# A decoder step on one core: in the recurrence's side work, the chunk products move ahead of the transpose of the decoded columns, and three pauses get longer

## The chip, the core and the metric

One core of a Trainium2 chip runs the whole program. The metric is the device time of one execution in microseconds (us); lower is better.

## The reference, cut to what is computed

One layer of a hybrid decoder, float32, for one prompt of 256 tokens and 8 decode rows (264 columns in all): a SwiGLU, a mixer, an attention over 256 memory tokens and a second SwiGLU, each with a layer norm behind it. The mixer is what matters here:

```python
proj = h @ p['w_in']                       # 2048 -> 3*1024 + 64 + 64 + 160 + 2*1024
r, k, v, wd, ad, gd = split(token_shift(proj[..., :SHIFT_COLS]))
# per head (16 heads of 64), per token t:
sa = einsum('bhvk,bhk->bhv', S, -kk_t)
S  = S * w_t[:, :, None, :] + sa[..., None] * (kk_t * a_t)[:, :, None, :] + v_t[..., None] * k_t[:, :, None, :]
y_t = einsum('bhvk,bhk->bhv', S, r_t)
o_a = ((group_norm(y) + bonus) * g)
u = glu(proj[..., SHIFT_COLS:])            # conv module: 31 taps along the tokens
o_b = silu(layer_norm(conv(u)))
merged = concatenate([o_a * beta_rwkv, o_b * beta_conv], -1) @ p['w_out']
```

## The kernel before, in words

Every weight matrix is read once, in chunks of 128x1024. ACT rounds a chunk to `whi` (L188) and DVE forms the rest `wlo` (L189); four such pairs are in store, three raw chunks ahead of them. Each product of activations and weights is three TensorE matmuls, `xh*whi`, `xl*whi` and `xh*wlo` (L303, L304, L305), 128x128 weights against 264 columns. I call these the large products and number them by their place on PE. A chunk is used by 24 of them.

The mixer first does the products with `w_in`, up to number 8784. As they go, 16 heads in four groups of four (g = 0 to 3) run the recurrence in chunked form as side work: small matmuls into one of four PSUM buffers (`mis`), with ACT and DVE work between them. For one group `rw_state` makes gates and scaled copies (`sig`, `a`, `E1`, `bk`, `ar`), the chunk products `G` (`gram`, L886, sixteen 128x128 matmuls, then four masked copies L890 on DVE), the transposed copies `bkT` (L825) and the solve of a triangular system, four rounds of L843 and L850 of 64 tiny matmuls each. `decode_rows` transposes the columns of the 8 decode rows (L1010) so that they can go through a DMA to `rw_decodes`. Then come the chain over the four chunks (`rw_chain`), the read (`rw_read`) and the group norm (`rw_out`, L1087 to L1106). The conv module's taps are DVE work (L1176), and its layer norm and Silu (`conv_apply`: L372 and L376 to L409, then L1200 and L1201) make the inputs k = 8 to 15 of the product with `w_out`.

That product, from number 8784, goes over four groups of 512 outputs. Within one it takes the inputs k = 0 to 5 (from groups 0 to 2), then 8 to 15 (conv). The inputs 6 and 7 come from group 3 and are taken last, from number 9288, so that group 3 can end in the meantime. Behind the product stand the residual (L1237, L1240, L1243) and the attention, whose memory rows come back by DMA (L1327) and are split again (L1328, L1329).

The order on each engine is set by the program. The main work yields a cost, which advances a clock `t`; each side has a time `next` at which it may issue its next piece, and a piece yields the pause until the following one:

```python
def step(self, now):
    self.next = now + self.pace * next(self.gen)
def pump(self):
    for s in self.sides:
        while not s.done and s.next <= self.t: s.step(self.t)
```

So a longer `yield` puts more large products ahead of what follows it. Before the product with `w_out` starts, groups 0 to 2 and the group norm of group 2 are issued to their ends (`self.finish(...)` in `mixer_out`); the sides of group 3 go on within it.

Of the kernel before, what the change touches and what calls it, by code (L numbers as in the profile page):

```python
# [12 lines left out]
ALU = mybir.AluOpType  # L13
# [14 lines left out]
C = 64  # L28
NC = TP // C
NP = 2 * NC  # L30
# [23 lines left out]
class Builder:  # L54
# [663 lines left out]
    def rw_state(self, g, S):  # L718

        nc = self.nc  # L720
        V, A = nc.vector, nc.scalar
# [15 lines left out]
        c8 = lambda t: t[:, :, :TP].rearrange("p i (c t) -> p i c t", t=C)  # L737
        e8 = lambda t, lo: t.rearrange("p (i c) t -> p i c t", i=2)[:, :, :, lo : lo + C]
# [38 lines left out]
        E1, E2 = L, Lc  # L777
# [11 lines left out]
        ar = S["ar"] = self.mt("ar", (128, NP, 2, C))  # L789
        bk = self.mt("bk", (128, 2, NC, 2, C))  # L790
        v8 = lambda t: t.rearrange("p (i c) t -> p i c t", i=2)
# [18 lines left out]
        r = S["r"]  # L810
        V.tensor_tensor(q[:, 1], q[:, 2], r[:, :, dec], ALU.mult)
        V.tensor_tensor(q[:, 5], a[:, :, dec], r[:, :, dec], ALU.mult)
        V.tensor_tensor(q[:, 6], k[:, :, dec], r[:, :, dec], ALU.mult)
        self.decode_rows(g, S)
        S["y"] = self.mt("y", (128, 2, T), bufs=2)
        self.decs.append(self.start(self.chain_after(self.decs[-1], self.rw_decodes(g, S)), DEC_PACE))
        V.tensor_tensor(v8(ar[:, :, 1]), c8(r), e8(E1, 1), ALU.mult)
        G = S["G"] = self.mt("G", (128, 2, NP, 2, C))
        self.gram(S)
        yield 1.0  # L820
        bkT = S["bkT"] = self.mt("bkT", (128, 2, NC, 128))
        for i in range(2):
            p = self.misc()
# [8 lines left out]
        mask = lambda l, o=slice(0, 128): self.lm[o, l, None].to_broadcast([o.stop - o.start, NP, B]).bitcast(I32)  # L832
        N = lambda n, c: G[QS[n], n // 2, c, 0, B * (n % 2) : B * (n % 2) + B]
        for n, o in enumerate(QS):
            V.copy_predicated(Q[o, :, 1], mask(0, o), N(n, slice(None)))
        V.transpose(Q[:, :, 0], Q[:, :, 1])
        yield 1.0
        b8 = lambda p: p[:, : B * NP].rearrange("p (c t) -> p c t", t=B)
        for l in range(1, 5):
            pp = b8(self.misc())  # L840
# [16 lines left out]
        for c in range(NP):  # L857
            for i in range(2):
                mm(pp[QS[2 * i + 1], c], G[QS[2 * i], i, c, 0, B:], Q[QS[2 * i], c, 0], start=True, stop=True)
        Pm = self.mt("P", (128, NP, B))  # L860
# [16 lines left out]
    def gram(self, S):  # L877
# [3 lines left out]
        for i in range(2):  # L881
# [7 lines left out]
            for h, p in enumerate(ps):  # L889
                nc.vector.tensor_tensor(  # L890
                    S["G"][:, i, NC * h : NC * h + NC],
                    p.rearrange("p c (a t) -> p c a t", t=C),
# [4 lines left out]
    def rw_chain(self, g, S):  # L897
# [17 lines left out]
        Z = S["Z"] = self.mt("Z", (128, NC + 1, 2, C))  # L915
        G, ar, bkT, QT = S["G"], S["ar"], S["bkT"], S["QT"]
        W2 = 2 * C
        h2 = lambda p: p[:, :W2].rearrange("p (h t) -> p h t", h=2)
        p = self.misc()
        for n in range(NP):  # L920
            for i in range(2):
                mm(p[HS[i], C * n : C * n + C], G[HS[1 - i], i, n, 0], UV[HS[1 - i], i, n], start=True, stop=True)
        W0 = self.mt("W0", (128, 2, NC, C))
# [41 lines left out]
    def rw_read(self, g, S):  # L965
# [14 lines left out]
        y = S["y"]  # L980
        G, ar, UV, Z = S["G"], S["ar"], S["UV"], S["Z"]
        p = self.misc()
# [891 lines left out]
```

## Time and profile before

| what | value |
|---|---|
| median of three runs | 2525.59 us (2519.16, 2527.02, 2525.59) |
| the profiled execution, its own time | 2526.33 us |
| span of its trace, first to last instruction | 2524.6 us |
| mean granted TensorE clock | 0.993 of full speed |
| PE busy | 2470.9 us, 98% |
| DVE, ACT, POOL busy | 1582.8, 1195.0, 261.7 us |
| products with `w_in` and the recurrence | about 840 to 1199 us of the span |
| product with `w_out` | about 1199 to 1340 us |

PE is busy nearly all the time, so the place to look is the stretches in which it is not, what released it there, and the granted clock. Matmuls are pipelined, so a row's duration is longer than its share of PE's time; large products follow each other every 0.12 us.

### The profile page before, as it was taken

The page shows a single profiled execution, that of the slowest core. Times are in us where ns is not written, and L with a number is a line of the kernel's source. Part 1 is how long each engine was busy: PE and PEld are TensorE (multiplying, and loading weights), DVE is VectorE, ACT ScalarE, POOL GpSimd, SP SyncE. Part 2 cuts the span into 40 slices and gives each one's busy share as a digit, 9 for nine tenths or more (in the row PEclk, how much of TensorE's full clock was granted, in tenths as well). Part 3 has the DMA queues.
Part 4 walks back from the last instruction along what each step waited for, and adds up shares of the span by engine and source line. Part 5 has one row for each costly group of instructions (what it writes and reads, how often), then busy time and mean ns, then how long its engine had stood idle before and what let it go on. Part 6 is the DMA issues. An engine that isn't in the chain of part 4 may idle for free. (4 is left out here: it accounts for less than half of the span.)

```text
span 2524.6 us, 53420 instructions
## 1 busy us (share of the span) xinstructions
PE 2470.9 (98%) x22328; PEld 2417.2 (96%) x22328; DVE 1582.8 (63%) x2545; ACT 1195.0 (47%) x1802; POOL 261.7 (10%) x422
## 2 busy tenths in 40 slices
PE   9999999999999999999989999999999999999998
PEld 9999999999999988988889888989999999999998
DVE  5545444444557599799777566789655545554465
ACT  5444433444446555455646354657444434444443
POOL 1300000000000001000110222220132500000000
PEclk9999999999999999999999999999999999999999
DMA  7656655555557754544476799976677755655554
GB/s 228 188 183 220 203 183 182 183 183 178 179 181 212 221 151 132 149 131 139 128 251 224 262 293 305 322 226 191 195 215 217 237 182 184 183 178 183 176 180 131
DMA packets 452211, 497.89 MB, mean 197 GB/s; under 512 B 22096, under 2 KB 418640, under 8 KB 451968
## 3 DMA queue, kind: packets, MB, share of 16 engines
q1 hardware_dynamic: 417840, 417.09, 54.0%
q0 software_dynamic: 20992, 67.22, 8.4%
q10 hardware_dynamic: 13136, 10.15, 1.2%
q8 instruction: 175, 2.87, 0.5%
q14 instruction: 68, 0.56, 0.1%
HBM read 477.76 MB, written 16.63 MB: 196 GB/s over the span
## 5 line engine op out<-in xcount | busy, mean ns | idle before, releaser
L189 DVE TENSOR_TENSOR wlo<-raw,whi 128x1024 fp32r<-128x1024 f32 (+1 forms) x791 | 961.4, 1216 | 850.6 <-ACT whi L188 847.3
L188 ACT ACTIVATE whi<-raw 128x1024 fp32r<-128x1024 f32 (+1 forms) x791 | 823.0, 1041 | 1035.6 <-PE acc L304 856.6
L303 PE MATMUL acc<-xh,whi 128*128 128x264 f32 x2864 | 828.7, 290 | 15.3 <-DVE y L1243 7.3
L304 PE MATMUL acc<-xl,whi 128*128 128x264 f32 x2864 | 820.2, 287 | 0.6 <-DVE xl L189 0.6
L305 PE MATMUL acc<-xh,wlo 128*128 128x264 f32 x2864 | 816.7, 286 | 0.5 <-DVE wlo L189 0.5
L303 PEld LDWEIGHTS acc<-xh,whi 128*128 128x128 f32 x2864 | 540.3, 189 | 23.8 <-ACT rh L1328 7.5
L304 PEld LDWEIGHTS acc<-xl,whi 128*128 128x128 f32 x2864 | 542.0, 189 | 3.7 <-DVE xl L189 0.8
L305 PEld LDWEIGHTS acc<-xh,wlo 128*128 128x128 f32 x2864 | 541.0, 189 | 2.3 <-DVE wlo L189 1.1
L303 PE MATMUL acc<-rh,whi 128*128 128x264 f32 (+2 forms) x1600 | 456.8, 285 | 0.2 <-ACT lnx L397 0.2
L305 PE MATMUL acc<-rh,wlo 128*128 128x264 f32 (+2 forms) x1600 | 454.5, 284 | 0.0
L304 PE MATMUL acc<-rl,whi 128*128 128x264 f32 (+2 forms) x1600 | 453.4, 283 | 0.0
L304 PE MATMUL acc<-gl,whi 128*128 128x264 f32 x1408 | 400.2, 284 | 0.0
L305 PE MATMUL acc<-gh,wlo 128*128 128x264 f32 x1408 | 400.1, 284 | 0.0
L303 PE MATMUL acc<-gh,whi 128*128 128x264 f32 x1408 | 399.5, 284 | 0.0
L303 PEld LDWEIGHTS acc<-rh,whi 128*128 128x128 f32 x1600 | 300.8, 188 | 2.2 <-ACT lnx L397 0.4
L304 PEld LDWEIGHTS acc<-rl,whi 128*128 128x128 f32 x1600 | 301.7, 189 | 1.2
L305 PEld LDWEIGHTS acc<-rh,wlo 128*128 128x128 f32 x1600 | 300.7, 188 | 0.2
L305 PEld LDWEIGHTS acc<-gh,wlo 128*128 128x128 f32 x1408 | 264.5, 188 | 0.1
L304 PEld LDWEIGHTS acc<-gl,whi 128*128 128x128 f32 x1408 | 264.5, 188 | 0.0
L303 PEld LDWEIGHTS acc<-gh,whi 128*128 128x128 f32 x1408 | 264.3, 188 | 0.1
L1176 DVE SCALAR_TENSOR_TENSOR y<-u,cw,y 128x256 f32<-128x256 f32 x240 | 111.1, 476 | 0.6
L397 ACT ACTIVATE lnx<-acc 128x264 f32<-128x264 f32 x84 | 32.4, 386 | 64.8 <-PE acc L305 64.8
(350 smaller groups left out, 2089.9 us busy)
## 6 DMA issues: line engine op xcount, KB each, us to landing
raw<-in_ffn_w SPq DMA_DIRECT2D x509, 512.0 KB, 3.6
raw<-in_w_in SPq DMA_DIRECT2D x86, 512.0 KB, 3.8
raw<-in_w_mk SPq DMA_DIRECT2D x32, 512.0 KB, 3.4
raw<-in_w_mv SPq DMA_DIRECT2D x32, 512.0 KB, 5.4
raw<-in_w_out SPq DMA_DIRECT2D x32, 512.0 KB, 5.1
kv<-in_cache_mem_k POOLq DMA_DIRECT2D x32, 512.0 KB, 6.2
raw<-in_w_mq SPq DMA_DIRECT2D x32, 512.0 KB, 5.2
kv<-in_cache_mem_v POOLq DMA_DIRECT2D x32, 512.0 KB, 6.1
```

Of the source, the lines that this page charges most:

```text
L188: a = self.nc.scalar.activation(hi, src, AF.Copy)
L189: return a, self.nc.vector.tensor_tensor(lo, src, hi.bitcast(F32), ALU.subtract)
L303: nc.tensor.matmul(out, wh, xh, start=start, stop=False)
L304: nc.tensor.matmul(out, wh, xl, start=False, stop=False)
L305: self.mark = nc.tensor.matmul(out, wl, xh, start=False, stop=stop)
L397: self.lastfn = self.nc.scalar.activation(*args, **kw)
L1176: V.scalar_tensor_tensor(c[:, :TP], u[:, i : i + TP], w(i), c[:, :TP], ALU.mult, ALU.add)
```

## The change

In `rw_state`, the product `ar[:, :, 1]` = r\*E1 (L817) and `gram` now come before `decode_rows`, with a pause of 2.2 between; the pause ahead of the `bkT` transposes is 2.4 instead of 1.0, and the one ahead of the solve 2.6 instead of 1.0. The chunk products used to follow the decoded columns with no pause.

```diff
@@ -811,13 +811,15 @@
         V.tensor_tensor(q[:, 6], k[:, :, dec], r[:, :, dec], ALU.mult)
+        V.tensor_tensor(v8(ar[:, :, 1]), c8(r), e8(E1, 1), ALU.mult)
+        yield 2.2
+        G = S["G"] = self.mt("G", (128, 2, NP, 2, C))
+        self.gram(S)
+
         self.decode_rows(g, S)
         S["y"] = self.mt("y", (128, 2, T), bufs=2)
         self.decs.append(self.start(self.chain_after(self.decs[-1], self.rw_decodes(g, S)), DEC_PACE))
-        V.tensor_tensor(v8(ar[:, :, 1]), c8(r), e8(E1, 1), ALU.mult)
-        G = S["G"] = self.mt("G", (128, 2, NP, 2, C))
-        self.gram(S)
-        yield 1.0
+        yield 2.4
         bkT = S["bkT"] = self.mt("bkT", (128, 2, NC, 128))
@@ -834,7 +836,7 @@
         V.transpose(Q[:, :, 0], Q[:, :, 1])
-        yield 1.0
+        yield 2.6
         b8 = lambda p: p[:, : B * NP].rearrange("p (c t) -> p c t", t=B)
```

Lines behind the change have numbers higher by two in the changed kernel (L886 becomes L888, L1010 becomes L1012); the text keeps the numbers of before. PE, DVE, POOL and SP issue the same instructions as before, in another order, and ACT two more table loads (L403). The table gives the number of large products ahead of each piece on PE, before and after:

| piece | group 0 | group 1 | group 2 | group 3 |
|---|---|---|---|---|
| L886, chunk products | 7317 -> 7318 | 7784 -> 7830 | 8282 -> 8337 | 8744 -> 8856 |
| L1010, decoded columns | 7312 -> 7318 | 7779 -> 7830 | 8277 -> 8342 | 8738 -> 8892 |
| L825, bkT | 7317 -> 7320 | 7784 -> 7836 | 8282 -> 8358 | 8744 -> 8916 |
| L843, first of the solve | 7339 -> 7358 | 7807 -> 7896 | 8304 -> 8394 | 8766 -> 8940 |
| last piece of the read (L998) | 7668 -> 7728 | 8166 -> 8256 | 8628 -> 8784 | 9001 -> 9057 |
| end of the group norm's products (L1105) | | | 8664 -> 8808 | 9018 -> 9085 |

From number 9564 on the orders are the same again.

On PE, group 0, rows of before, then of the change (`L303` to `L305` are large products, `mis` the PSUM buffers; the rows of L886 between those shown are alike):

```order
L303 MATMUL acc_10568<-xh_9078,whi_10523 128x264
L1010 MATMUL mis_10584<-ident,q_10379 80x128
L304 MATMUL acc_10568<-xl_9094,whi_10523 128x264
...
L304 MATMUL acc_10567<-xl_9095,whi_10523 128x264
L305 MATMUL acc_10567<-xh_9079,wlo_10524 128x264
L886 MATMUL mis_10594<-ar_10476,bk_10477 128x128
...
L825 MATMUL mis_10637<-ident,bk_10477 128x128 x4
L825 MATMUL mis_10643<-ident,bk_10477 128x128 x4
L303 MATMUL acc_10568<-xh_9079,whi_10523 128x264
```

```order
L303 MATMUL acc_10568<-xh_9079,whi_10523 128x264
L888 MATMUL mis_10626<-ar_10476,bk_10477 128x128
...
L1012 MATMUL mis_10650<-ident,q_10379 80x128
L304 MATMUL acc_10568<-xl_9095,whi_10523 128x264
L305 MATMUL acc_10568<-xh_9079,wlo_10524 128x264
L827 MATMUL mis_10693<-ident,bk_10477 128x128 x4
L827 MATMUL mis_10699<-ident,bk_10477 128x128 x4
```

The chunk products come a single large product later than before, the decoded columns stand behind them, and `bkT` two products behind those.

On ACT, at the entry into the product with `w_out`, rows of before, then of the change (`lnvar`, `lnrs` belong to the conv module's layer norm, `y` and `xh` with L1200 are its Silu and the input k = 8; `sig`, `q`, `a`, `t_`, `L` are group 3's gates; `r` with L397 is the group norm of group 2):

```order
L188 ACTIVATE whi_15302<-raw_15030 128x1024
L376 ACTIVATE lnvar_15313<-mis_15308 128x264
L397 ACTIVATE lnrs_15314<-lnvar_15313,eps_150 128x264
L397 ACTIVATE lnrs_15314<-lnrs_15314 128x264
L403 ACT_TABLE_LOAD
L188 ACTIVATE whi_15399<-raw_15145 128x1024
L845 ACTIVATE P_15460<-mis_15427 128x256
L397 ACTIVATE y_9731<-y_9731,mv 128x264
L1200 ACTIVATE xh_15113<-y_9731,mv 128x264
```

```order
L188 ACTIVATE whi_14993<-raw_14732 128x1024
L397 ACTIVATE r_13227<-mis_14891,eps_154 128x264
...
L1101 ACTIVATE y_13612<-y_13612,mv 128x264 x2
L397 ACTIVATE sig_14948<-mis_14956,mv 128x4x64
...
L782 ACTIVATE t_2122_14952<-a_14951,omka,mv 128x264 x2
L397 ACTIVATE t_2123_14953<-t_2123_14953 128x528
...
L188 ACTIVATE whi_15046<-raw_14776 128x1024
...
L376 ACTIVATE lnvar_15057<-mis_15052 128x264
...
L188 ACTIVATE whi_15114<-raw_14919 128x1024
L397 ACTIVATE lnrs_15058<-lnvar_15057,eps_150 128x264
...
L397 ACTIVATE y_9731<-y_9731,mv 128x264
L1202 ACTIVATE xh_14847<-y_9731,mv 128x264
```

Before, the gates of group 3 and the group norm of group 2 are long past when the layer norm of the conv module comes; in the change they stand ahead of it, from number 8808 on. The input k = 8 is wanted at number 8856 in both.

On DVE, at the end of group 3 (L1240 and L1243 are the residual; L1329 splits the memory rows that were loaded again), before, then the change:

```order
L189 TENSOR_TENSOR wlo_16061<-raw_15974,whi_16060 128x1024
L1240 SCALAR_TENSOR_TENSOR y_16338<-y_16338,lnc_15896 128x264
...
L1329 TENSOR_TENSOR rl_16474<-rl_16474,rh_16458 128x256
...
L189 TENSOR_TENSOR wlo_16091<-raw_16004,whi_16090 128x1024
L1243 TENSOR_TENSOR y_15878<-y_15878,acc_15906 128x264
```

```order
L1242 SCALAR_TENSOR_TENSOR y_15886<-y_15886,lnc_15898 128x264
L189 TENSOR_TENSOR wlo_16093<-raw_16006,whi_16092 128x1024
L1245 TENSOR_TENSOR y_15880<-y_15880,acc_15908 128x264
...
L189 TENSOR_TENSOR wlo_16131<-raw_16036,whi_16130 128x1024
L1242 SCALAR_TENSOR_TENSOR y_16340<-y_16340,lnc_15898 128x264
...
L1331 TENSOR_TENSOR rl_16476<-rl_16476,rh_16460 128x256
```

L1243, which frees the accumulators that PE needs at number 9120, stood behind splits of reloaded memory rows and now stands ahead of them.

## Rows read from the trace of the kernel before

**Rows 1.** From the page: busy time, share of the span and instructions of each engine.
```profile
PE 2470.9 (98%) x22328; PEld 2417.2 (96%) x22328; DVE 1582.8 (63%) x2545; ACT 1195.0 (47%) x1802; POOL 261.7 (10%) x422
```

**Rows 2.** Groups of PE's instructions by line, from 850 to 1300 us: line, operation, tiles and shape, count, busy us and mean ns of one, then the idle us of PE just before them and what ended it.
```profile
L303 PE MATMUL acc<-xh,whi 128*128 128x264 f32 x793 | 238.2, 303 | 7.6 <-DVE y L1243 7.3 <-ACT xh L1200 0.2
L850 PE MATMUL mis<-P,Q 32*32 32x32 f32 x1024 | 13.3, 197 | 5.2 <-issue 4.2 <-ACT P L845 1.1
L843 PE MATMUL mis<-Q,G 32*32 32x32 f32 x1024 | 12.5, 196 | 3.5 <-DVE Q L836 3.2
L825 PE MATMUL mis<-ident,bk 128*128 128x128 f32 x32 | 5.0, 286 | 3.0 <-DVE G L890 3.0
L1010 PE MATMUL mis<-ident,q 128*80 128x128 f32 x4 | 1.1, 278 | 3.5 <-DVE q L811 3.5
```

**Rows 3.** Timeline of PE in groups 0 and 2: start us, duration us, instruction, count, and in brackets the idle time before it with its releaser.
```profile
903.30 0.28 PE L1010 MATMUL mis<-ident,q 128*80 128x128 f32 x1 [1.98 <-DVE q L811]
...
1100.73 0.74 PE L843 MATMUL mis<-Q,G 32*32 32x32 f32 x64 [0.90 <-DVE Q L836]
...
1104.59 0.44 PE L850 MATMUL mis<-P,Q 32*32 32x32 f32 x16 [1.88 <-issue]
1104.96 0.59 PE L304 MATMUL acc<-xl,whi 128*128 128x264 f32 x1
...
1105.56 0.42 PE L303 MATMUL acc<-xh,whi 128*128 128x264 f32 x1
```

**Rows 4.** Stretches of 50 us: length, busy us (and count) of PE, PEld, DVE, ACT and POOL, the granted TensorE clock as a share of full speed, the DMA share and GB/s.
```profile
1100.00:1150.00 50.00, 47.39 (x932) 43.26 (x932) 44.14 (x100) 22.84 (x46) 2.50 (x5) 0.93 0.53 145
1200.00:1250.00 50.00, 47.66 (x773) 41.11 (x773) 40.08 (x98) 30.26 (x54) 6.98 (x13) 0.97 0.45 143
1250.00:1300.00 50.00, 42.68 (x343) 41.61 (x339) 31.11 (x61) 22.82 (x39) 13.13 (x23) 0.93 0.71 238
```

**Rows 5.** Timeline of DVE in group 0, columns as in rows 3.
```profile
903.00 0.16 DVE L811 TENSOR_TENSOR q<-q,r 128x16 f32<-128x16 f32 x1
...
903.26 0.68 DVE L817 TENSOR_TENSOR ar<-r,L 128x512 f32<-128x512 f32 x1
903.86 1.21 DVE L189 TENSOR_TENSOR wlo<-raw,whi 128x1024 fp32r<-128x1024 f32 x1
```

**Rows 6.** Timeline of ACT, the gates of group 3 and the group norm of group 2, columns as in rows 3.
```profile
1165.89 0.47 ACT L397 ACTIVATE sig<-mis,mv 128x256 f32<-128x256 f32 x1
...
1169.52 0.84 ACT L397 ACTIVATE a<-mis,mv 128x264 f32<-128x264 f32 x2
1170.37 1.28 ACT L403 ACT_TABLE_LOAD   x1
1171.67 0.85 ACT L397 ACTIVATE r<-mis,eps 128x264 f32<-128x264 f32 x2
1172.55 0.65 ACT L397 ACTIVATE r<-r 128x528 f32<-128x528 f32 x1
1173.11 1.09 ACT L782 ACTIVATE t<-a,omka,mv 128x264 f32<-128x264 f32 x2
...
1175.67 0.62 ACT L397 ACTIVATE L<-sig 128x520 f32<-128x520 f32 x1
...
1182.88 1.04 ACT L188 ACTIVATE xh<-y 128x264 fp32r<-128x264 f32 x3
```

**Rows 7.** Timeline of ACT at the layer norm of the conv module, columns as in rows 3.
```profile
1207.28 1.06 ACT L188 ACTIVATE whi<-raw 128x1024 fp32r<-128x1024 f32 x1 [0.33 <-PE acc L304]
1208.24 0.38 ACT L376 ACTIVATE lnvar<-mis 128x264 f32<-128x264 f32 x1
1210.57 0.52 ACT L397 ACTIVATE lnrs<-lnvar,eps 128x264 f32<-128x264 f32 x1 [1.96 <-DVE lnvar L378]
...
1211.56 1.28 ACT L403 ACT_TABLE_LOAD   x1
1212.85 1.06 ACT L188 ACTIVATE whi<-raw 128x1024 fp32r<-128x1024 f32 x1
...
1214.25 0.61 ACT L397 ACTIVATE y<-y,mv 128x264 f32<-128x264 f32 x1
1214.89 0.51 ACT L1200 ACTIVATE xh<-y,mv 128x264 fp32r<-128x264 f32 x1
```

**Rows 8.** Timeline of DVE at that layer norm (its work between the last `lnrs` of ACT and the Silu), columns as in rows 3.
```profile
1211.72 0.43 DVE L388 SCALAR_TENSOR_TENSOR lnvar<-lnvar,lnrs 128x264 f32<-128x264 f32 x1
```

**Rows 9.** Timeline of PE at the end of the recurrence, columns as in rows 3: the group norm of group 3 and the wait for accumulators.
```profile
1254.26 1.16 PE L1093 MATMUL mis<-k,blk 128*128 128x264 f32 x4
1257.28 0.48 PE L303 MATMUL acc<-xh,whi 128*128 128x264 f32 x1
1277.38 0.56 PE L303 MATMUL acc<-xh,whi 128*128 128x264 f32 x1 [7.32 <-DVE y L1243]
1281.04 0.36 PE L304 MATMUL acc<-xl,whi 128*128 128x264 f32 x1
```

**Rows 10.** Timelines of ACT and DVE there, columns as in rows 3.
```profile
1273.92 0.78 ACT L1328 ACTIVATE rh<-rl 128x256 fp32r<-128x256 f32 x2 [1.31 <-DMA rl<-mem]
...
1262.02 1.46 DVE L1240 SCALAR_TENSOR_TENSOR y<-y,lnc 128x264 f32<-128x264 f32 x4
1276.82 1.44 DVE L1243 TENSOR_TENSOR y<-y,acc 128x264 f32<-128x264 f32 x4
```

## The prediction, made before the changed kernel ran

> **What bounds the kernel.** I read the page first: PE is busy for 98% of the span [rows 1], so a change of order can only win or lose where PE is idle or runs slowly. The groups of PE's instructions between 850 and 1300 us then show where the idle time lies, and the reader should look at the column behind the second bar [rows 2]. The small products of the recurrence wait 3.5 us at L1010 (the decoded columns), 3.0 at L825 (bkT), 3.5 at L843 and 5.2 at L850, which is 15.2 us over the four groups; the chunk products (L886) have no row of their own there because they never wait. The large products lose 7.6 us, nearly all in one wait for L1243. So 22.8 us is all that lies open here, and ten of it, 3.5 + 3.0 + 3.5, belongs to the three kinds of small products that the change pushes back. The granted clock is the third view: it falls to 0.93, 0.97 and 0.93 in three stretches [rows 4]. In the timeline the large products behind the 1.88 us wait follow each other at 0.22 us, not at 0.12 [rows 3]: this is the lower of the clock's two levels (1.2 and 2.4 GHz), after a PE that stood idle twice in 5 us, 0.90 and 1.88. That costs 0.1 us a product, some 24 products, so 2.4 us; the same behind the 7.32 us wait lasts from 1277.38 to 1281.04, 17 products, 1.7 us [rows 9].
>
> **The change, part by part.** Instructions do not change, but for two table loads on ACT, so every term is a wait. All durations are those of the one profiled execution, 2526.33 us; I sum against that.
>
> *Groups 0 to 2.* In group 0 L1010 waits 1.98 us for L811, the first of four DVE instructions that stand in a row behind a `wlo`; L817, which the chunk products need, is the fourth and ends at 903.94 [rows 3, 5]. In the change L886 is at that place, one large product later than before, so it meets the same DVE row: PE, idle from 901.32, gets there six products later, at 902.04, and with 0.14 us from DVE's end to PE's start, as at L1010, it waits until 904.08. The wait of 2.0 is moved, not removed. L1010 behind it needs a fifth `mis` buffer while the chunk products hold all four, and L890 on DVE frees one only after a `wlo` of 1.21 us [rows 5]: I take 1.3 for L1010 and L825, and 0.3 for L843. In groups 1 and 2, by walking down DVE's order with these durations, L886 waits 0.8 and 1.3, L1010 and L825 together 0.9 and 0.9, and the solve 0.75 and 0. With 0.7 of issue waits that is 9.0. The bounds: 4 (the pauses work in groups 1 and 2 as the order has it, where 52 to 90 more products, 6 to 11 us, lie ahead of L825 and L843 now) and 14 (each L886 waits as in group 0).
>
> *Group 3.* It is moved whole into the product with `w_out`, where its solve, chain and group norm stand within 150 large products instead of 280. I take 2.5 us of data waits and 2.0 of issue waits, between 1.5 and 8, by the mean of 3.8 us a group in rows 2. Groups 0 to 3 together: 9.0 + 4.5 - 15.2 = **-1.7**.
>
> *The entry into the product with w_out.* This is the largest term, and it is new. From number 8808, where PE frees the split's buffer, ACT must now do in one row, before the input k = 8 for number 8856: three splits (0.96 start to start), 2.9; the group norm of group 2, 1.45 and 1.1; two table loads of 1.3, 2.6; the sigmoids 1.0 and 0.85; L782, 1.0; four exponentials and logarithms 2.3; two `xh` 0.7; `lnvar` and two copies 0.7; `lnrs` 1.0 [rows 6, 7]. That is 15.6. Then DVE has nine small instructions at about 0.34 start to start and a `wlo` of 1.15 between `lnrs` and the Silu, 4.2 [rows 8], beside which the third load lies, and Silu and `xh` take 1.1 [rows 7]: 20.9 us. PE has 48 large products in that time, 5.8; the group norm's products, 2.3 (from 3.0 with L349 in it [rows 9]); the gates' small ones, 2.1; the layer norm's 0.9; eleven of L886, 1.4: 12.5. PE waits for the difference, **+8.4**. For the seven inputs that follow, DVE has 13.9 us of work (1.1 an input, three `wlo`, four masked copies) beside 12.3 on PE: **+1.6**. Before, the gates and the group norm had been done some 30 us earlier [rows 6, 7] and nothing waits here for more than 0.2 [rows 2]. Bounds of both: 0, if DVE and ACT run ahead, and 16, if every DVE step within the row stops ACT too.
>
> A rule of the Trainium skill speaks against this change here. The rows show that ACT's next instruction starts 1.3 us after a table load's start, right at its end of 1.28 [rows 6, 7], and I count 1.3. The Trainium skill, page "ScalarE: Activation LUTs", section "What ACT_TABLE_LOAD costs", says that a switch costs the load and about 1380 ns of draining, 2.66 us in all. By it the two loads in the row would make the entry 2.8 us longer, as an estimate; the trace does not agree, since no gap follows the loads.
>
> *The clock.* With the two waits of group 2 apart, the half-rate stretch at 1105 us goes: **-2.4**, between -2.4 and 0. The one behind 7.32 us stays in kind but comes behind the entry's 8.4 as well: **+1.7**, between 0 and +10.
>
> *The end of group 3.* PE waits 7.32 us at number 9120 for accumulators that L1243 frees; L1243 starts at 1276.82 behind a `wlo` whose split stands behind reloaded memory rows (L1328) [rows 9, 10]. In the change it stands ahead of them. But the group norm ends at number 9085, 67 products later, and what follows on DVE (from PE's 1257.28 to the end of L1240 at 1263.48, a `wlo`, a first L1243: 8.0 us) outlasts the 35 products that PE has left, 4.2: it waits 3.8, and 0.5 more comes at a later split behind the reload. **-3.0**, between -7 and +3.
>
> *Fewer pieces.* The small products stand in 135 separate places instead of 140, at about 0.2 us each: **-1.0**.
>
> Sum: -1.7 + 8.4 + 1.6 - 2.4 + 1.7 - 3.0 - 1.0 = +3.6, so 2526.33 + 3.6 = 2529.9. The median of the runs shown is 0.7 lower than the profiled execution, less than I can resolve; I predict **2530.0 us**.
>
> **Rivals.** About 0.3%, 7.6 us, is what a measurement of this kernel can tell from no change: below 2518.0 is faster, above 2533.2 slower.
>
> *Faster: the pauses do what their order says.* More products lie ahead of L825 and L843 in groups 1 to 3, ACT is idle for half of the time here (23 us busy of 50, where DVE has 44 [rows 4]), and the entry's row is shortened because ACT takes the gates while PE still does the group norm. Then the ten of the three kinds, 2.4 of the clock, 3.0 and 1.0 go, and half of the entry, 5.0, remains: 2526.3 - 16.4 + 5.0 = 2514.9; with a third of the ten left 2518. Against it: ACT's row is one chain, with its first step tied to PE's number 8808.
>
> *Slower: the low clock lasts through the squeezed group 3.* PE now stops at the entry, at L886, at several inputs, in the solve and at number 9120. The trace charges 1.7 to 2.4 us for each stretch at half rate [rows 3, 9]. If four such stops stand far enough apart to cost that each, in place of the one I count, the price is 3 x 1.7 to 3 x 2.4, 5 to 7 more: 2535 to 2537, and with the entry at 13 instead of 10, 2540. It decides by whether the granted clock of the product with `w_out` stays above 0.93. For it: two waits of 0.90 and 1.88 within 5 us were enough before.
>
> *No change of place for the waits.* What DVE owes to the small products is the same work; the wait only changes its line, as in group 0, and group 3's end swallows both signs: 2523 to 2529.
>
> *Table loads that drain.* If a load cost a further 1.3, 2.6 more at the entry: 2532.5. The Trainium skill, page "ScalarE: Activation LUTs", would have it so.
>
> **How the numbers follow.** The forecast gets 0.40; with an error of some 6 us about it, 0.27 lies within the bound, 0.12 above it and 0.01 below. The faster rival 0.20, the slower one 0.22, the moved waits 0.15, the draining loads 0.03 (0.02 within, 0.01 above). Faster: 0.01 + 0.20 = 0.21. Slower: 0.12 + 0.22 + 0.01 = 0.35. Same: 0.27 + 0.15 + 0.02 = 0.44. For the range I leave out a tenth at each end: half of the faster rival lies below 2516, and of the slower one the upper part, with all of its stops and a long entry, above 2541. The likeliest case alone, the forecast with its error, runs from 2524 to 2536.
>
> **What would show it.** Right, if L886 in group 0 has a wait of about 2 us; if the first large product with the input k = 8 (released by `xh` L1200, or by the Silu ahead of it) waits between 5 and 10 us; if the stretch 1100 to 1150 is granted 1.00 and the one behind the entry less; and if the wait for L1243 has gone down to about 4. Wrong, if no wait above 3 us stands at the entry, if L1243's wait is still 7, or if waits of L825 and L843 fall to nearly nothing in all groups.

## The result, and the profile after

| | before | changed kernel |
|---|---|---|
| median of five runs | 2524.57 us (2517.59 to 2527.02) | 2536.99 us (2535.73 to 2542.90) |
| span of the profiled execution | 2524.6 us | 2535.3 us |
| mean granted TensorE clock | 0.993 | 0.991 |

The ratio is 1.0063, 95% interval 1.0049 to 1.0078: slower by 0.63%; the medians differ by 12.4 us. That is the way the forecast pointed (+3.6 us, 2530.0) and inside its range (2516 to 2541), but over three times its size, and it is what the slower rival named, 2535 to 2537.

First the groups of PE's instructions of the changed kernel, 850 to 1350 us, columns as in [rows 2]; lines are higher by two.

```profile
L303 PE MATMUL acc<-xh,whi 128*128 128x264 f32 x879 | 263.0, 303 | 10.0 <-DVE y L1245 8.2 <-ACT xh L1202 1.2 <-DVE v L701 0.4
L845 PE MATMUL mis<-Q,G 32*32 32x32 f32 x1024 | 12.8, 194 | 5.0 <-issue 3.7 <-DVE Q L838 1.3
L852 PE MATMUL mis<-P,Q 32*32 32x32 f32 x1024 | 12.6, 197 | 3.2 <-ACT P L847 1.7 <-issue 1.5
L888 PE MATMUL mis<-ar,bk 64*128 64x128 f32 x128 | 10.0, 306 | 7.0 <-DVE bk L795 5.6 <-DVE ar L814 1.3
L827 PE MATMUL mis<-ident,bk 128*128 128x128 f32 x32 | 4.3, 276 | 0.0
L1012 PE MATMUL mis<-ident,q 128*80 128x128 f32 x4 | 1.1, 285 | 3.3 <-DVE G L892 3.3
```

The pauses did what they say for two of their three targets: bkT (L827) no longer waits, 3.0 before, and the solve's first product (L845) waits 1.3 us for DVE instead of 3.2. But L888, which never waited, now waits 7.0, and L1012 behind it has 3.3, hardly less than the 3.5 before, only with the chunk products' PSUM copies (L892) as the releaser. So the 9.7 us that the three kinds waited for DVE before have become 11.5 at these lines and L888.

The timeline of PE shows where: at the entry into the product with `w_out`, and at two waits for accumulators.

```profile
1203.66 2.71 PE L888 MATMUL mis<-ar,bk 64*128 64x128 f32 x21 [5.09 <-DVE bk L795]
1207.76 1.25 PE L303 MATMUL acc<-xh,whi 128*128 128x264 f32 x4 [1.18 <-ACT xh L1202]
...
1285.05 0.39 PE L303 MATMUL acc<-xh,whi 128*128 128x264 f32 x1 [3.10 <-DVE y L1245]
...
1312.38 0.56 PE L303 MATMUL acc<-xh,whi 128*128 128x264 f32 x1 [5.07 <-DVE y L1245]
1312.74 0.42 PE L304 MATMUL acc<-xl,whi 128*128 128x264 f32 x1
```

The single wait of 7.32 us [rows 9] has become two, 3.10 and 5.07. Each row of the first pair also tells of the clock: 21 records of L888 in 2.71 us, where group 0 has 28 in 1.83, and four L303 in 1.25 us, where the kernel `a_dummy` below has 0.75. The stretches say how long, columns as in [rows 4]:

```profile
900.00:950.00 50.00, 44.96 (x880) 41.78 (x879) 47.07 (x103) 22.19 (x41) 5.37 (x11) 0.97 0.58 163
1100.00:1150.00 50.00, 47.11 (x908) 44.08 (x904) 47.46 (x104) 25.26 (x47) 4.29 (x9) 1.00 0.58 166
1200.00:1250.00 50.00, 40.12 (x793) 34.93 (x795) 36.45 (x80) 24.51 (x44) 8.48 (x16) 0.82 0.38 125
1250.00:1300.00 50.00, 46.88 (x422) 42.07 (x419) 26.34 (x64) 22.69 (x44) 13.17 (x23) 0.94 0.47 157
1300.00:1350.00 50.00, 44.94 (x349) 44.48 (x348) 40.89 (x83) 21.66 (x33) 0.00 (x0) 0.93 0.61 209
```

The stretch 1100 to 1150 is granted 1.00 now (0.93 before), as forecast. But 1200 to 1250 has 0.82. A stretch of 50 us at granted clock c has lost (1 - c) x 50 us of work, if PE was busy: before, 3.5 + 1.5 + 3.5 = 8.5 us; now 1.5 + 9.0 + 3.0 + 3.5 = 17.0 (the stretches from 900 on that are not shown are granted 1.00). In the 9.0 and 3.0 lie two spells at half rate of 10.2 us each, from 1201 to 1211 and from 1242 to 1252 us, and a third of 3.4.

**The account.** A landmark behind all of this is the layer norm's first product behind the product with `w_out`, L372 at 1333.45 us before and 1348.38 now, +14.9:

```profile
1333.45 0.68 PE L372 MATMUL mis<-lns,ones 128*128 128x264 f32 x2
```
```profile
1348.38 0.68 PE L372 MATMUL mis<-lns,ones 128*128 128x264 f32 x2
```

PE's idle time from 900 to there went from 22.8 to 30.7 us, +7.9; the clock loss by +8.5. Their sum, 16.4, is the landmark's shift but for 1.5 us, of which some 0.8 is half-rate time that lies within the waits and so is counted twice. From there to the end of the span the changed kernel was 4.2 us quicker; that part scatters from run to run (1180.8 to 1192.0 us over the kernels below, whose orders there are nearly all the same), so I read the landmark, not the end.

### The profile page after: what moved, and what is told of

It is laid out like the page before. It is cut to its first block, busy times and chain, and to the rows that moved or that the text cites. A ratio compares the mean times of both kernels' runs of the same rounds, so it can differ in the third digit from the quotient of the medians.

```text
span 2535.3 us, 53435 instructions
## 1 busy us (share of the span) xinstructions
PE 2479.1 (98%) x22328; PEld 2424.8 (96%) x22328; DVE 1583.5 (62%) x2545; ACT 1196.6 (47%) x1804; POOL 262.2 (10%) x422
## 4 chain that ended last, share of the span: by engine, by line
PE 83%; DVE 6%; DMA 5%; ACT 3%; issue 3%; POOL 0%; ACTq 0%; SPq 0%; POOLq 0%; DVEq 0%
PE acc L303 26%; PE acc L305 26%; PE acc L304 26%; DVE wlo L189 2%; DVE y L1178 1%; ACT whi L188 1%; DMA raw<-in_w_mv 1%; DMA raw<-in_ffn_w 1%; DMA raw<-in_w_mq 1%; DMA raw<-in_w_mo 1%; PE mis L1459 0%; PE mis L1474 0%; DMA rl<-mem 0%; PE mis L852 0%; PE mis L845 0%
## 5 line engine op out<-in xcount | busy, mean ns | idle before, releaser
L303 PE MATMUL acc<-xh,whi 128*128 128x264 f32 x2864 | 828.8, 291 | 15.6 <-DVE y L1245 8.2
L305 PE MATMUL acc<-xh,wlo 128*128 128x264 f32 x2864 | 817.9, 286 | 0.5 <-DVE wlo L189 0.5
L303 PEld LDWEIGHTS acc<-xh,whi 128*128 128x128 f32 x2864 | 541.2, 190 | 24.7 <-issue 5.8
L305 PEld LDWEIGHTS acc<-xh,wlo 128*128 128x128 f32 x2864 | 541.7, 189 | 2.5 <-DVE wlo L189 0.9
L303 PE MATMUL acc<-rh,whi 128*128 128x264 f32 (+2 forms) x1600 | 457.3, 286 | 0.1
L305 PE MATMUL acc<-rh,wlo 128*128 128x264 f32 (+2 forms) x1600 | 455.9, 285 | 0.0
L305 PE MATMUL acc<-gh,wlo 128*128 128x264 f32 x1408 | 400.1, 284 | 0.0
L303 PE MATMUL acc<-gh,whi 128*128 128x264 f32 x1408 | 399.5, 284 | 0.0
L303 PEld LDWEIGHTS acc<-rh,whi 128*128 128x128 f32 x1600 | 301.3, 188 | 2.3 <-issue 0.3
L305 PEld LDWEIGHTS acc<-rh,wlo 128*128 128x128 f32 x1600 | 301.2, 188 | 0.2
L305 PEld LDWEIGHTS acc<-gh,wlo 128*128 128x128 f32 x1408 | 264.5, 188 | 0.1
L303 PEld LDWEIGHTS acc<-gh,whi 128*128 128x128 f32 x1408 | 264.3, 188 | 0.1
L397 ACT ACTIVATE lnx<-acc 128x264 f32<-128x264 f32 x84 | 32.4, 386 | 66.0 <-PE acc L305 66.0
```

The lines of the kernel that those rows point to most:

```text
L303: nc.tensor.matmul(out, wh, xh, start=start, stop=False)
L305: self.mark = nc.tensor.matmul(out, wl, xh, start=False, stop=stop)
L397: self.lastfn = self.nc.scalar.activation(*args, **kw)
```

## The experiments

The ratio is to runs of the kernel before that were timed beside each; idle is PE's, 900 to 1350 us, in waits above 0.15 us; clock loss is (1 - granted clock) x 50 us summed over nine stretches from 900; both, and the landmark L372, are from the one profiled execution.

| kernel | ratio (95%) | idle | clock loss | idle + clock, against before | landmark, against before |
|---|---|---|---|---|---|
| before | 1 | 22.8 | 8.5 | | |
| change | 1.0063 (1.0049, 1.0078) | 30.7 | 17.0 | +16.4 | +14.9 |
| order_only | 1.0007 (0.9994, 1.0019) | 24.8 | 8.5 | +2.0 | +1.1 |
| long_g3 | 1.0006 (0.9994, 1.0017) | 25.1 | 3.0 | -3.2 | -0.5 |
| a_pace80 | 1.0029 (1.0012, 1.0047) | 25.2 | 10.0 | +3.9 | +1.9 |
| order_22 | 1.0048 (1.0031, 1.0065) | 28.3 | 16.5 | +13.5 | +13.4 |
| a_dummy | 1.0044 (1.0027, 1.0061) | 27.0 | 9.5 | +5.2 (and 6 of extra work) | +10.7 |
| a_spread | 1.0040 (1.0025, 1.0055) | 30.5 | 13.5 | +12.7 | +14.0 |
| a_kv | 1.0045 (1.0030, 1.0060) | 31.2 | 15.5 | +15.4 | +13.2 |
| a_spread_kv | 1.0049 (1.0033, 1.0066) | 33.6 | 15.0 | +17.3 | +17.5 |
| a_gate | 1.0025 (1.0010, 1.0040) | 27.6 | 10.0 | +6.3 | +9.1 |
| b_kv | 0.9985 (0.9976, 0.9995) | 22.9 | 3.5 | -4.9 | -3.5 |
| b_spread_kv | 0.9986 (0.9975, 0.9998) | 20.6 | 5.0 | -5.7 | -0.8 |
| b_gate | 0.9973 (0.9957, 0.9988) | 19.5 | 1.5 | -10.3 | -7.7 |

The two columns on the right agree within 2.8 us, but for a_dummy, whose extra work is not idle, and b_spread_kv, where 4.9 us are unaccounted for. So idle time and low clock are an account of what these edits do, to within some 3 us. The profiled executions of b_kv and b_gate were the fastest of their runs, 3.5 and 7.8 us below the medians, so their last two columns are not those of a usual run.

**The order without the pauses.**

```diff
-        yield 2.2
         G = S["G"] = self.mt("G", (128, 2, NP, 2, C))
...
-        yield 2.4
+        yield 1.0
...
-        yield 2.6
+        yield 1.0
```

> The changed kernel with its order (chunk products ahead of the transpose of the decoded columns) but with the pauses of before: no pause ahead of the chunk products, 1.0 and 1.0 behind them. Group 3 then stands where it did, its chunk products behind 8744 large products, its group norm ends at 9018. Theory A, the loss comes from group 3 being pushed into the product with w_out: about 2524.6, within 3 us of before, no wait above 1 us at L888 in group 3, and the wait for L1245 is 7 us as before. Rival B, the swap itself costs, because four chunk products hold all four small buffers and L1012 behind them must wait: the waits of L888 and L1012 together stay near 4.6 us as in the change and the time is 2530 or more.

2527.73 us, no difference from before that can be told. L888 and L1012 wait 6.97 us together in its four groups, which is more than rival B wanted; but L1010 and L825 waited 6.5 us before, L825 has 0.5 now, and L843 waits 2.3 for DVE instead of 3.2. So the waits have only moved, and B, which wanted 2530 or more, falls. The wait at number 9120 is 7.74 us.

**The order and the pause of 2.2.** The last two pauses are 1.0 again.

> The order of the change and its pause of 2.2 ahead of the chunk products, the other two pauses 1.0 as before. Group 3's gates stand behind 8712 large products (before 8628, change 8808), its chunk products behind 8792 (8744, 8856). If the loss goes with the number of products by which group 3 is late (theory A, linear), it is 84 of 180 of the 12.4 us, 5.8 us: 2530. If it comes only once the gates stand behind the group norm of group 2 and beside the layer norm of the conv module on ACT (theory A, threshold), the wait of L888 in group 3 is under 1 us, and the time is 2523 to 2527. Under rival B (the swap costs) 2530 or more, with waits at L888 and L1012.

2535.33 us. Neither reading held. The entry's wait is gone (L888 in group 3 waits 0.47 us), as the threshold wanted, but the time is nearly that of the whole change, more than the linear reading gives. Its idle time is spread over some twenty waits of 0.3 to 3.1 us, two of the longest for issue in the solves of groups 0 and 1 (3.12 and 2.38), and the clock loss is as large as in the change, most of it between 1217 and 1251 us, where group 3's solve and chain stand. So a loss of this size doesn't need the one wait at the entry: here it comes from many stops.

**All pauses at 0.8**, which puts group 3 back.

```diff
-HEAD_PACE, DEC_PACE, OUT_PACE, CONV_PACE, ATT_PACE = 1.0, 0.85, 1.49, 1.0, 1.0
+HEAD_PACE, DEC_PACE, OUT_PACE, CONV_PACE, ATT_PACE = 0.8, 0.85, 1.49, 1.0, 1.0
```

> The changed kernel with every pause of the recurrence's side multiplied by 0.8 (HEAD_PACE), which keeps the new order and the new ratio of the pauses, but puts group 3 back where it stood: gates behind 8622 products, chunk products behind 8748, group norm ending at 9026 (before 8628, 8744, 9018). Theory A (group 3's place is what costs): 2522 to 2527, no wait above 1 us at the entry into the product with w_out and one wait for L1245 of about 7 us. Rival: the longer pauses themselves cost by more separate pieces or by waits at L845 and L852 in groups 0 to 2, then 2530 or more.

2529.42 us, 1.0029: a little over half of the loss is gone, not all of it. It missed the range of theory A, and just missed the rival's 2530. The entry has a wait of 2.03 us for a conv input, not under 1 as expected, and the wait for L1245 is 4.47 where about 7 was expected.

**The longer pauses in group 3 alone.**

```diff
+        if g == 3:
+            yield 2.2
...
+        yield 2.4 if g == 3 else 1.0
...
+        yield 2.6 if g == 3 else 1.0
```

> The order of the change in all groups, its three longer pauses in group 3 alone; groups 0 to 2 have the pauses of before. Group 3's gates then stand at 8628 and its chunk products at 8744 as in the kernel before, its solve begins behind 8779 products (8766 before), its group norm ends at 9028 (9018). If the 0.29% that the kernel with all pauses at 0.8 kept comes from groups 0 to 2 (more issue waits and a half-rate stretch in group 0, behind the pause of 2.6), this one is within 3 us of before, 2521 to 2527, and group 0 has no half-rate stretch. If it comes from group 3's solve standing close, it is 2528 or more, with waits of 2 us or more at L852 and at the conv inputs near number 8856.

2524.67 us, no difference from before; the stretch 900 to 950 is granted 1.00. So the loss needs the longer pauses of groups 0 to 2; they act on group 3 because each group starts behind the one before, and in a_pace80, whose group 3 is back in place, they still seem to cost something, though the two intervals touch. In group 0 of a_pace80 the second round of the solve waits 1.75 us for issue and the stretch 900 to 950 has 0.97; the kernels with the change's pauses there have 0.34 to 3.79, before had 0.88, long_g3 1.66. That is too uneven to build on.

**Thirteen extra matmuls in the entry's wait**, queued behind the last large product ahead of it.

```diff
         def ready(k):
+            if k == 8 and self.fill:
+                self.fill = False
+                with self.hold():
+                    warm = self.misc()
+                    for _ in range(13):
+                        self.nc.tensor.matmul(warm[:, :T], self.blk, self.wdad, start=True, stop=True)
             want = order.index(k)
```

> The changed kernel with 13 extra matmuls of 128x264, whose result nothing reads, on PE at number 8856, in the place where it waits 5.1 us for group 3's bk. Theory C: the low clock costs something of its own there. The wait shrinks to about 0.5 us, no half-rate stretch follows, the chunk products behind take 2.1 us instead of 2.9 and the large products 0.12 us instead of 0.22: 2 to 4 us lower, 2533 to 2535. Rival: after the wait PE is bound by ACT's and DVE's conv inputs anyhow and a faster clock is waited away: 2537 within 1 us, with longer waits at the inputs k = 8 to 12; or the extra products end late and it is 1 us slower.

2535.24 us. The timeline of its PE at the entry, and its two stretches:

```profile
1198.68 5.95 PE L1309 MATMUL mis<-wdad,blk 128*128 128x264 f32 x26
1204.56 1.83 PE L888 MATMUL mis<-ar,bk 64*128 64x128 f32 x28
1208.03 0.75 PE L303 MATMUL acc<-xh,whi 128*128 128x264 f32 x4 [1.64 <-ACT xh L1202]
```
```profile
1200.00:1250.00 50.00, 42.95 (x856) 37.29 (x855) 37.95 (x82) 26.77 (x48) 8.48 (x16) 0.97 0.40 125
1250.00:1300.00 50.00, 46.87 (x414) 42.68 (x413) 28.89 (x72) 20.53 (x40) 13.16 (x23) 0.97 0.55 183
```

The extra work (26 records for 13 matmuls) fills the wait to its end and about 0.6 us beyond (L888 starts 9.8 us behind L372 here, 9.2 in the change). L888 has 28 records in 1.83 us where it had 21 in 2.71, four L303 take 0.75 instead of 1.25, and the spell at half rate at the entry is gone. From 1200 to 1220 us, the change, then a_dummy:

```profile
1200.00:1220.00 20.00, 15.05 (x105) 13.92 (x105) 17.94 (x43) 11.94 (x22) 2.67 (x5) 0.74 0.34 116
1200.00:1220.00 20.00, 16.22 (x123) 14.32 (x122) 18.73 (x45) 12.83 (x23) 3.94 (x8) 1.00 0.39 122
```

But nothing is gained by that there. From number 8856 to 8916 the change takes 11.56 us without a wait, 3.7 of them at half rate; a_dummy takes 11.84, and the last 2.14 of these are a wait for the next conv input:

```profile
1219.87 0.51 PE L303 MATMUL acc<-xh,whi 128*128 128x264 f32 x2 [2.14 <-ACT xh L1202]
```

So at the entry it went as the rival of the expectation has it: ACT and DVE set the pace, and the faster clock is waited away.

The landmark comes 4.3 us earlier than in the change all the same. That arises from number 8952 to 9000, in the solve and behind it, where the edit does nothing: 16.1 us here, 22.3 in the change, 10.2 of them at half rate. Four kernels below, a_spread, a_kv, a_spread_kv and a_gate, have the same order on PE as the change up to number 9120, and their half-rate spell here is 3.4 us. These are the 20 us from 1240 on in the change, in those four and in a_dummy:

```profile
1240.00:1260.00 20.00, 19.99 (x224) 16.82 (x224) 5.49 (x10) 9.09 (x18) 0.00 (x0) 0.74 0.17 60
1240.00:1260.00 20.00, 18.77 (x294) 15.75 (x294) 5.88 (x12) 9.09 (x18) 0.00 (x0) 0.91 0.24 80
1240.00:1260.00 20.00, 18.89 (x241) 15.88 (x240) 5.88 (x12) 9.40 (x20) 0.00 (x0) 0.91 0.23 77
1240.00:1260.00 20.00, 17.56 (x335) 14.66 (x334) 5.86 (x11) 9.01 (x19) 0.00 (x0) 0.91 0.25 81
1240.00:1260.00 20.00, 18.49 (x290) 15.47 (x290) 5.89 (x13) 9.40 (x19) 0.00 (x0) 0.91 0.24 81
1240.00:1260.00 20.00, 19.90 (x268) 16.36 (x268) 6.80 (x17) 10.70 (x21) 0.00 (x0) 1.00 0.30 102
```

Without its waits, the work from number 8952 to 9000 takes 19.5 us with 10.2 at half rate, 16.6 to 16.7 with 3.4, and 15.1 with none. Here, then, the low clock is a cost of its own, a little under half of its time. Why the spell was 10.2 us long in the change's profile and 3.4 in four others behind much the same waits isn't shown, nor whether a_dummy's edit took it away. By the runs a_dummy gains 1.7 us, and the intervals overlap.

**The second wait for accumulators.** Three edits, first alone, then together. One spreads the splits of the reloaded memory rows:

```diff
             self.nc.gpsimd.dma_start(raw, self.mkeep[:, k])
-            self.nc.scalar.activation(hi, raw, AF.Copy)
-            self.nc.vector.tensor_tensor(lo, raw, hi.bitcast(F32), ALU.subtract)
+        self.reload = self.start(self.mem_split())
...
+    def mem_split(self):
+        for k in range(KD):
+            hi, lo = self.mh[k][:, :TP], self.ml[k][:, :TP]
+            with self.tc.issue_after(self.pulse[0].ins), self.tc.issue_after(self.pulse[1].ins):
+                self.split_from(lo.bitcast(F32), hi, lo)
+            yield 1.2
...
+        b.finish(b.reload)
```

> The changed kernel, with the splits of the reloaded memory rows (L1330, L1331) issued one by one in the course of the product with w_out, each queued behind the chunk split last issued, instead of all at once; their DMAs as before. Theory R: the 5.07 us wait for L1245 at the last inputs is due to these splits, which hold up the chunk splits on DVE and ACT and so the raw chunks behind them. Then that wait falls below 1 us, the stretch at half rate behind it goes, and the time is 5 to 8 us lower: 2529 to 2532. Rival: the wait is for the raw chunks of w_out themselves (the DMAs are late whatever DVE does), then it stays above 3 us and the time stays within 2 us of 2537. The wait of 3.1 us at number 9120, behind the group norm, stays under both.

The wait fell from 5.07 to 3.02 us, not below 1. The median of 2537.91 shows no gain, and the interval of the ratio overlaps the change's. Theory R has a share at most.

The second moves four loads to another queue:

```diff
-            self.nc.sync.dma_start(self.kv_dest(u)(), self.kv_rows(o, cg))
+            self.nc.gpsimd.dma_start(self.kv_dest(u)(), self.kv_rows(o, cg))
```

> The changed kernel with the four loads of early keys and values (n<-out) issued from POOL's queue, behind the reload of the memory rows, instead of from SP's, where they stand ahead of chunks of w_out and wait until the group norm of group 3 frees the mixer's memory (4.8 us in the change, 8.7 in before). Theory S: those loads on SP are what makes the chunks late, and so the wait of 5.07 us for L1245. Then it falls below 2 us, ACT waits less than 2 us for a chunk of w_out in place of 6.5, and the time is 3 to 6 us lower: 2531 to 2534. Rival R: the splits of the reloaded rows alone hold the chunks up, then it stays above 4 us and the time within 2 us of 2537.

The wait stayed, 5.91 us. Theory S alone falls.

> Both: the splits of the reloaded rows spread out, as in the run before with 3.0 us left of that wait, and the early keys and values on POOL's queue. If each has a share (S and R together), the second wait for L1245 falls below 0.5 us, and with it the half-rate stretch behind: 5 to 8 us below the change, 2529 to 2532. If the chunks are late for another reason (three raw buffers only), 2 to 3 us of it stay. The wait of 3.1 us at number 9120 behind the group norm is not touched by either.

3.81 us are left, and 0.54 at the next accumulator: not half a microsecond as two shares would give. Something else made the chunks late. The DMA view of this kernel, 1290 to 1312 us, shows a candidate (KB each, median us from issue to landing): five loads of the key cache run in the same stretch as the chunks of `w_out` and take 11.2 us at the median.

```profile
raw<-in_w_out SPq DMA_DIRECT2D x5, 512.0 KB
kv<-in_cache_mem_k POOLq DMA_DIRECT2D x5, 512.0 KB, 11.2
n<-out POOLq DMA_DIRECT2D x4, 256.0 KB, 6.0
```

The third holds these loads back, by an ACT instruction that writes to their tiles first:

```diff
+                if len(tiles) < KV_BUFS:
+                    with self.tc.issue_after(self.pulse[0].ins):
+                        nc.scalar.activation(t[:, 0, 0:1], self.ident[:, 0:1], AF.Copy)
                 nc.gpsimd.dma_start(t, src)
```

> The changed kernel with the splits of reloaded rows spread out, the early keys and values on POOL's queue, and now also the first five loads of the key cache (512 KB each) held back until attention begins. Theory W: the second wait for L1245 is left because everything that waits for the mixer's memory is loaded at once when group 3 ends, and the chunks of w_out then land in 7 us instead of 4 beside it. Then with the cache loads out of the way the wait of 3.8 us falls below 1.5 us, and ACT no longer waits 3 us for a chunk. Rival: L1245 stands on DVE behind six chunk splits that PE itself frees too late (four buffers), then 3 us or more stay. Total in the first case 2528 to 2532, in the second 2534 to 2537; the first scores of attention may wait a few us for their loads and take that back.

The timeline of its PE at the same two places:

```profile
1284.86 0.39 PE L303 MATMUL acc<-xh,whi 128*128 128x264 f32 x1 [3.09 <-DVE y L1245]
...
1313.51 0.36 PE L303 MATMUL acc<-xh,whi 128*128 128x264 f32 x1 [0.52 <-DVE y L1245]
```

The second wait is 0.52 us, the first is untouched, and the median 2529.67, 1.0025. Theory W holds for PE's wait: what waits for the mixer's memory is loaded all at once when group 3 ends, and the chunks that L1245 stands behind come late beside it. ACT still waits 2.94 us for one chunk, which should have gone too. Whether holding back the cache loads alone would do, without the first two edits, wasn't tried.

**The same edits on the kernel before.**

> The kernel before with the early keys and values on POOL's queue. Its wait of 7.32 us for L1243 ends behind a chunk split that stands on ACT behind reloaded rows; if those rows alone set it (R), the wait stays between 6 and 8 us and the time within 2 us of 2524.5; if the chunk load behind n<-out on SP sets it (S), it falls below 4 and the time by 3 to 5 us.

2518.98 us, 0.9985. The wait for L1243 at number 9120 is 6.22 us, as R has it, and there are no half-rate stretches at 1105 and 1217 us in this execution, so the gain isn't shown to come from the queue.

> The kernel before with both edits, the splits of the reloaded rows spread and the early keys and values on POOL's queue. The wait of 7.32 us should fall to the tail of the group norm (about 0 to 2 us, since the group norm ends 102 products ahead of number 9120), and the half-rate stretch behind it should go, 1.7 to 2.4: 2515 to 2519, faster than both kernels. If the wait only moves to a later accumulator, as it did in the change, 2521 to 2525.

2518.95 us, 0.9986. The 7.32 became 2.60, 2.21 and 0.53 at three accumulators: partly moved on.

> The same three edits on the kernel before. The waits for L1243 were 2.6, 2.2 and 0.5 us with the first two edits alone. If the cache loads crowd the chunks (W), the last two go and the total is 2514 to 2518; if the key cache then comes late to attention, 2519 to 2524.

2516.08 us, 0.9973 (0.9957 to 0.9988): faster than both kernels, with waits of 2.42 and 0.53 for L1243 and a clock loss of 1.5 us. Of the last two waits of b_spread_kv the 2.21 is gone, the 0.53 stays. The key cache did not come late enough to take the gain back. One and the same chunk of `w_out`, issued among the cache loads in b_spread_kv (DMA view, 1277.3 to 1277.6 us) and without them in b_gate (1274.75 to 1274.85), shows what they cost:

```profile
raw<-in_w_out SPq DMA_DIRECT2D x1, 512.0 KB, 9.8
```
```profile
raw<-in_w_out SPq DMA_DIRECT2D x1, 512.0 KB, 4.0
```

## Why the prediction came out as it did

The direction and the range were right, but one step failed: the clock, priced at -0.7 us; and the end of group 3 came with the wrong sign. The entry, 3.0 us below its forecast, and 4.2 us that came back behind the landmark, where no term stood, made up for a part of both. So the time lies inside the range in part by luck.

- **Groups 0 to 2: a reason held, the size was off.** The wait moved from L1010 to L888 in group 0 (1.27 us, forecast 2.0, against 1.98), with 1.30 for L1012 behind the full PSUM buffers (forecast 1.3 with L825). The sum over the three groups is 11.4 us, forecast 9.0 and 11.0 before. In groups 1 and 2 L888 waits less than walked (under 0.15 and 0.49, where 0.8 and 1.3 were forecast). The miss is in the issue waits, 1.72 us in group 0's solve and 0.95 in group 2's, where I had counted on 0.7 in all.
- **The entry: the row right, the place and the size in part.** The forecast was +8.4 for the row on ACT and DVE and 1.6 for the inputs behind. The row came as walked: the Silu starts behind DVE's tail and the large products for k = 8 right behind `xh`. The waits are 5.09 + 1.18 + 0.22 + 0.48 = 7.0 us. But the sign I had named, a wait of 5 to 10 us at k = 8, did not come: 5.09 stands just ahead, at L888, for group 3's `bk`, where the forecast had counted work on PE and no wait, and k = 8 itself waits 1.18. Most of the difference to 10 is the slow clock, at which PE's own work takes longer: at the higher level, in a_dummy, the waits behind L888 are 1.64 and 2.14, which with the 5.09 makes 8.9. This is the timeline of ACT there; it gives the term's last steps:

```profile
1201.61 0.42 ACT L397 ACTIVATE lnrs<-lnrs 128x264 f32<-128x264 f32 x1
1201.94 0.20 ACT L805 ACTIVATE q<-a 128x16 f32<-128x16 f32 x1
1202.16 1.28 ACT L403 ACT_TABLE_LOAD   x1
1206.56 0.61 ACT L397 ACTIVATE y<-y,mv 128x264 f32<-128x264 f32 x1 [3.11 <-DVE y L409]
1207.19 0.52 ACT L1202 ACTIVATE xh<-y,mv 128x264 fp32r<-128x264 f32 x1
```

- **The table loads: right as counted.** In the row, the two loads are followed at once by the next ACT instruction, 1.29 and 1.30 us after their start:

```profile
1188.30 1.28 ACT L403 ACT_TABLE_LOAD   x1
1189.59 0.61 ACT L1101 ACTIVATE y<-y,mv 128x264 f32<-128x264 f32 x1
...
1193.20 1.28 ACT L403 ACT_TABLE_LOAD   x1
1194.50 1.11 ACT L782 ACTIVATE t<-a,omka,mv 128x264 f32<-128x264 f32 x2
```

  The rule of the Trainium skill, page "ScalarE: Activation LUTs", section "What ACT_TABLE_LOAD costs", which adds a drain of about 1380 ns to a load, does not agree with these rows either.
- **Group 3's waits: right.** 4.2 us (0.21, 0.69, 0.54, 0.89, 0.38, 1.51), forecast 4.5.
- **The end of group 3: half right.** The wait at number 9120 is 3.10 us, forecast 3.8. But "0.5 more comes at a later split behind the reload" was 5.07. I had looked at the splits' place on ACT and DVE, not at the chunks' loads, which compete with 2.5 MB of cache loads that the same event lets go:

```profile
1306.11 1.06 ACT L188 ACTIVATE whi<-raw 128x1024 fp32r<-128x1024 f32 x1 [6.54 <-DMA raw<-in_w_out]
```

  This term came out at +0.9 (8.2 against 7.3) where -3.0 was forecast.
- **The clock: the step that failed.** The forecast took one half-rate stretch off and put one on, -0.7 together. The trace has +8.5. (The two are not counted alike: by the granted clock the stretches that I priced at 2.4 and 1.7 come to 3.5 each, and a third, at 1217 us, 1.5 before and gone now, had no term.) Group 2's stretch did go, but 1201 to 1211 and 1242 to 1252 us ran at half rate, the first from within the wait of 5.09 on, the second behind six waits of 0.2 to 1.5 us within 16 us in the solve of group 3. I had written this down as the slower rival, priced at 5 to 7 us more, and gave it 0.22; it is what the trace shows, 9.2 more. What each spell was worth differs: that at the entry could be taken away without a gain, as a_dummy shows, and that in the solve cost 4.4 us of PE's time (19.5 against 15.1). The Trainium skill, page "TensorE: Matmul & The Clock Gate", section "Terms", prices time at a lowered clock at that time times the share of the clock that is missing; the account above does the same, and the trace agrees within 2.8 us for all kernels but two.
- **What stays open:** of the change's 12.4 us, a_dummy and a_gate give back parts (1.7 and 7.3 by the medians), and no run has both. Why all pauses at 0.8 keep nearly half of the loss, with group 3 back in its place, is open too. What makes the issue waits in the solve so uneven, 0.34 to 3.79 us at the same place of the same order, wasn't tried.

## What to carry to other kernels

A pause that hides a small product's wait also delays all that comes behind it: look where the last of such chains ends, and what stands there already. On a PE that is 98% busy, price a new wait as its idle time plus what is lost at half rate behind it, and ask first whether another engine sets the pace there: then a faster clock is only waited away. Short waits close together can bring the low clock as a long one does. And where many loads wait for the same memory, ask what else is on the DMA engines in the moment that they are let go.

## What the runs showed of the hardware

Three things I had not expected. Several waits of 0.2 to 1.5 us within 16 us were followed by 10.2 us at the lower of the two clock levels, as long a spell as at a single wait of 5.09 us; but behind much the same waits in the same order the spell was 3.4 us in four other executions. Six microseconds of matmuls that nothing reads, put into the wait of 5.09 us, kept the higher level there (granted clock 1.00 instead of 0.74 from 1200 to 1220 us) and cost no time: the large product for k = 8 starts 13.3 us behind L372 in both kernels. And loads of 2.5 MB from one queue delayed chunk loads on another: ACT waited 6.54 us for a chunk, and a chunk among such loads took 9.8 us to land in b_spread_kv, where the median of 13 chunks in the kernel before, 1180 to 1240 us, was 5.1.
